# Seven block products in place of eight for the first four K-blocks of the up projection, in five of eleven column pairs of a decoder layer

## The chip, the core and the metric

The kernel runs on one core of a Trainium2 chip. The metric is the time of one execution on the device in microseconds (us). Before the change three runs took 1396.29, 1396.41 and 1396.53 us (median 1396.41).

## What is computed

One layer of a decoder on 256 tokens of width 2048: a normalisation, a combined input projection, two branches (a gated delta rule and a block attention) that sigmoid gates merge, an output projection, and then the part that matters here, a gated MLP with a short causal convolution behind its up projection:

```python
h = rms_norm(x, ln2[l])
u = causal_dwconv(h @ w_up[l], ffn_conv[l], ffn_conv_bias[l])
u_gate, u_val = jnp.split(u, 2, axis=-1)
x = x + (jax.nn.silu(u_gate) * u_val) @ w_down[l]
```

`h` is 256 x 2048, `w_up` is 2048 x 11264 (5632 columns of gate, 5632 of value), `w_down` is 5632 x 2048, all in float32.

## The kernel before

**Matrix products in three parts.** A float32 operand is split into a high and a low part that TensorE (PE) multiplies at full speed: `split` (L103) has ScalarE (ACT) write the high part with a CAST (L104) and VectorE (DVE) the low part with a TENSOR_TENSOR that subtracts (`low`, L101). A block product is then three matmuls (high times high, low of the activations times high of the weights, high times low), called products below. Each has 128 tokens x 128 K as its stationary operand and 128 K x 512 columns as its moving one. All go through `main_mm` (L93), which also counts them and, about every eight of them, calls `tick`: this lets each generator in the list `bg` record a little of its background work.

**Weights.** `fetch` (L112) loads 1 MB of a weight, 128 x 2048, through SyncE's (SP's) queue into one of four buffers `wraw`. Each half of it, 128 x 1024, is split into a slot of the ring `wh`/`wl`, which has four slots; a half in its slot is called a part here. The cast of a part waits until PE has finished with the part four places earlier, so ACT and DVE run at most three parts ahead of PE.

**Up projection (697.7 to 1161.8 us).** `by_token` (L190) makes 512 columns at a time, for both halves of the tokens, in two banks of PSUM. There are 22 such column blocks, gate and value in turn, so eleven pairs. A block has 16 K-blocks; a part holds two K-blocks, so a part gives PE 2 K-blocks x 2 token halves x 3 = 12 products, and a pair has 16 parts and 192 products. The accumulator pool has six banks as three turning pairs, and two more banks for small things.

**Behind each column block** ACT empties the two banks (`ut`, L1000), and a background generator `convolved` (L968) turns the result into channels on partitions: DVE transposes (`xt`, L468), SP issues 16 small DMAs (`uc`, L473), and then the convolution runs on each of four channel blocks, one ACT operation (L954) and two on DVE (L956). For a gate block ACT applies Silu (`sgt`, L978); for a value block (`cvf`) GpSimd (POOL) multiplies it by the gate and writes `acts`, 44 channel blocks of 128 x 256, the input of the down projection. A second generator, `residual_turned`, turns `x1`, the residual, through ACT's DMA queue.

**Down projection (from 1161.8 us).** It has 22 steps for each of two halves of the columns. In eleven of these 44 steps the function `seven` (L1035) does a 2 x 2 block product with seven block products in place of eight: DVE adds blocks of weights and of activations, the sums are split like weights, and `folds` (L1070) adds the accumulators.

**Order.** The text of the program is not the order on the engines. A scheduler places the instructions on each engine; what it chose is fixed in the program, and each engine runs its own list strictly in order, waiting by semaphores. So an instruction that waits holds up all that stand behind it on its engine.

Of the kernel before, what the change touches and what calls it, by code (L numbers as in the profile page):

```python
# [11 lines left out]
F32 = mybir.dt.float32  # L12
# [15 lines left out]
EPS = 1e-6  # L28
EVERY = 1700
SHIFT = 72  # L30
SEVEN = ([7, 10, 13, 15, 17], [2, 4, 7, 9, 12, 14])
# [34 lines left out]
def layer_kernel(ctx: ExitStack, tc: tile.TileContext, xT, xw, pos, cst, ceye, vec, convw, ffw, bdv,  # L66
# [8 lines left out]
    def r3(t, b):  # L75
        return t.rearrange("p (a b) -> p a b", b=b)
# [12 lines left out]

    spent = [0]  # L90

    def main_mm(ps, a, b, start, stop):
        r = pe.matmul(ps, a, b, start=start, stop=stop, skip_group_check=True)  # L93
# [9 lines left out]
    def split(hi, lo, src):  # L103
        casts.append(act.copy(hi, src))  # L104
        return low(hi, lo, src)
# [5 lines left out]

    def fetch(src, n=2048):  # L112
        raw = wpool.tile([P, 2048], F32, name="wraw", tag="wraw", bufs=4)
        sp.dma_start(raw[:, :n], src)
        return raw

# [8 lines left out]
    def load_w(src, o, ol=None, into=(None, None), raw=None, order=(0, 1)):  # L125
        raw = raw or fetch(src)
        w = [None, None]
        for h in order:
            w[h] = into[h] or parts(o, ol)
            lows.append(split(*w[h], raw[:, 1024 * h:1024 * h + 1024]))  # L130
        return w
# [23 lines left out]
    def mmt(name):  # L155
        return pst[0].tile([P, 2, 2, T] if wide[0] is True else [P, 2, T], F32, name=name, tag="mm")

    def sdt(name):
        return pst[1].tile([P, 512], F32, name=name, tag="sd")
# [30 lines left out]
    def by_token(ws, x, kt, name):  # L190

        if wide[0] is True:
# [743 lines left out]
    m_st.close()  # L936
    wide[0] = 2
    psum_pools(6, 2)

    b = bk.enter_context(tc.tile_pool(name="b2", bufs=2, reuse_waits="tile"))  # L940
# [19 lines left out]
    def convolved(n, ut):  # L960
# [18 lines left out]

    bg.append(residual_turned())  # L980
    pd = [None] * 8
    banks = [[2, 3, 6, 7], [0, 1, 4, 5]]

    def accumulators(n):
        for i in range(2):
            pd[n + i] = mmt("pd").rearrange("p a b -> p (a b)")

    def residual_in(p, i):
        for h in range(2):
            n = 2 * p + h  # L990
            act.copy(r3(pd[banks[p][2 * i + h]], P), x1[:, 4 * n:4 * n + 4, i * P:i * P + P])

    for n in range(NF // 2):
        if n == NF // 2 - 1:
            accumulators(2)
            residual_in(0, 0)
        ps = by_token(w_up[4 * ((n % 2) * 11 + n // 2):][:4], h2, KD, "ps_up")
        ut = ub.tile([P, 4, 2, P], F32, name="ut", bufs=2)
        for i in range(2):
            act.activation(ut[:, :, i, :], r3(ps[i], P), AF.Identity, scale=R2c[:, i:i + 1])  # L1000
        bg.append(convolved(n, ut))
    accumulators(6)
    residual_in(0, 1)
    accumulators(4)
    pd[:2] = sdt("pd"), sdt("pd")

    NQ = NF // 2
    LAST = 3
# [26 lines left out]
    def seven(c, m, q, a, raw, start, stop):  # L1035
# [6 lines left out]
        b1 = [t[:, :512] for t in b1]  # L1042
        lows.append(split(*b1, blk(raw, 0)))
        lows.append(split(*b2, raw[:, 1024:]))
        for to, more in ((0, 1), (1, 3), (3, 0), (2, 3)):
            dve.tensor_tensor(blk(raw, to), blk(raw, to), blk(raw, more), op=ALU.add)
        with tc.issue_after(lows[-1].ins):
# [3 lines left out]
        split(*s_, S)  # L1051
        split(*t13, raw[:, :1024])
        split(*t42, raw[:, 1024:])

# [31 lines left out]
    for p in range(2):  # L1086
# [3 lines left out]
        if p:  # L1090
            residual_in(1, 0)
            residual_in(1, 1)
        for q in range(NQ):
# [16 lines left out]
            for h in range(2):  # L1110
                lows.append(split(*w[h], blk(raw, h, 1024)))
            if last:
# [118 lines left out]
```

## Time and profile before

| | |
|---|---|
| median of three runs | 1396.41 us |
| the profiled execution, whole | 1396.18 us |
| its span, first to last instruction | 1394.4 us |
| granted clock of TensorE over the span | 0.999 |
| busy: PE, weight load, DVE, ACT, POOL | 99%, 86%, 74%, 57%, 10% |
| the up projection on the chain that ended last | 33% (ps_up) |

A profile page of this kind shows one execution. Busy shares are averages over very different stages; which engine sets the end is read from the chain of waits and from what PE, the busiest engine, waited for. Matmuls overlap in the records: one is listed with 380 ns, but the next begins 220 ns after it. DVE and ACT operations overlap a little as well, so their list of starts tells more than the sum of their durations.

### The profile page before, as it was taken

What the parts mean: (1) busy time and instruction counts of PE and PEld (TensorE: products, weight loads), DVE (VectorE), ACT (ScalarE), POOL (GpSimd) and SP (SyncE); (2) the same over time, 40 slices, a digit from 0 to 9 for tenths busy, and PEclk for the clock granted to TensorE, in tenths of its full rate; (3) what the DMA queues carried; (4) which work ended last, traced back from release to release, by engine and by line L of the source; (5) the groups of instructions that cost most, each with busy time, mean ns of one, the idle gap of its engine ahead of it and who ended that gap; (6) DMA issues with size and microseconds to landing.
All of it is one profiled execution on the core that took longest, in us unless ns stands there. A gap on an engine that the chain in (4) does not pass through costs nothing.

```text
span 1394.4 us, 19606 instructions
## 1 busy us (share of the span) xinstructions
PE 1384.0 (99%) x7222; PEld 1202.1 (86%) x7222; DVE 1026.5 (74%) x1500; ACT 792.9 (57%) x987; POOL 137.9 (10%) x116
## 2 busy tenths in 40 slices
PE   9999999999999999999999999999999999999997
PEld 8998899888888888889988888888888888888886
DVE  7988886988564446766756676676766667999995
ACT  6765545645466544445556555555565566666763
POOL 0021000200001100001100111100111101700000
PEclk9999999999999999999999999999999999999999
DMA  9566653576546555776557677786786776746561
GB/s 367 183 208 220 212 198 130 184 224 243 197 134 214 207 190 187 236 255 216 209 164 262 190 237 230 200 268 208 220 267 209 216 264 211 265 170 240 184 247 67
DMA packets 204673, 297.41 MB, mean 213 GB/s; under 512 B 167096, under 2 KB 169536, under 8 KB 172064
## 3 DMA queue, kind: packets, MB, share of 16 engines
q1 hardware_dynamic: 184656, 288.73, 61.5%
q10 hardware_dynamic: 17840, 3.67, 1.4%
q0 software_dynamic: 2080, 3.75, 0.9%
q8 instruction: 56, 0.92, 0.3%
q14 instruction: 41, 0.34, 0.1%
HBM read 273.48 MB, written 3.15 MB: 198 GB/s over the span
## 4 chain that ended last, share of the span: by engine, by line
PE 97%; DMA 1%; DVE 1%; SPq 0%; issue 0%; ACT 0%; DVEq 0%; ACTq 0%
PE ps_up L93 33%; PE pd L93 16%; PE ps_gate L93 12%; PE ps_gdn L93 9%; PE ps_wo L93 6%; PE ps_moba L93 6%; PE ps_br L93 5%; PE ps_v L93 3%; PE ps_z L93 3%; PE g L81 1%; DMA wraw<-in_w_o 1%; PE ps_gdn L260 1%; DMA xs<-in_xw 0%; SPq L856 0%; PE po L81 0%; PE sc L747 0%
## 5 line engine op out<-in xcount | busy, mean ns | idle before, releaser
L101 DVE TENSOR_TENSOR wl<-wraw,wh 128x1024 fp32r<-128x1024 f32 (+1 forms) x476 | 578.9, 1220 | 290.2 <-ACT wh L104 282.3
L104 ACT CAST wh<-wraw 128x1024 fp32r<-128x1024 f32 (+1 forms) x476 | 491.3, 1037 | 441.9 <-PE ps_up L93 142.2
L93 PE MATMUL ps_up<-wh,h 128*128 128x512 f32 x1408 | 422.8, 380 | 0.2 <-DVE x L916 0.2
L93 PEld LDWEIGHTS ps_up<-wh,h 128*128 128x128 f32 x1408 | 264.1, 188 | 46.0 <-issue 0.6
L93 PE MATMUL ps_up<-wl,h 128*128 128x512 f32 x704 | 267.6, 380 | 0.0
L93 PE MATMUL ps_gate<-wh,hc 128*128 128x512 f32 x512 | 155.4, 382 | 0.0
L93 PEld LDWEIGHTS ps_up<-wl,h 128*128 128x128 f32 x704 | 132.1, 188 | 22.7
L93 PE MATMUL ps_gdn<-hc,wh 128*128 128x256 f32 x720 | 124.2, 276 | 0.0
L973 POOL TENSOR_TENSOR acts<-sgt,cvf 128x256 f32<-128x256 f32 x44 | 79.3, 1812 | 448.6 <-DVE cvf L956 372.0
L93 PEld LDWEIGHTS ps_gate<-wh,hc 128*128 128x128 f32 x512 | 95.8, 188 | 16.4
L93 PEld LDWEIGHTS ps_gdn<-hc,wh 128*128 128x128 f32 x720 | 108.4, 188 | 1.3 <-issue 0.6
L93 PE MATMUL ps_gdn<-hc,wl 128*128 128x256 f32 x360 | 97.9, 275 | 0.0
L93 PE MATMUL ps_gate<-wl,hc 128*128 128x512 f32 x256 | 97.8, 382 | 0.0
L93 PE MATMUL ps_wo<-mc,wh 128*128 128x512 f32 x256 | 85.7, 379 | 0.8 <-DVE gts L886 0.8
L93 PE MATMUL pd<-tt,ah 128*128 128x512 f32 x282 | 82.2, 380 | 0.0
L93 PE MATMUL ps_moba<-wh,hc 128*128 128x512 f32 x256 | 77.1, 381 | 0.0
L93 PE MATMUL ps_wo<-mc,wl 128*128 128x256 f32 x256 | 70.5, 276 | 0.0
L93 PEld LDWEIGHTS ps_gdn<-hc,wl 128*128 128x128 f32 x360 | 67.1, 188 | 0.3
L104 ACT CAST tt<-wraw 128x1024 fp32r<-128x1024 f32 x46 | 47.4, 1045 | 33.8 <-PE pd L93 20.6
L93 PEld LDWEIGHTS pd<-tt,ah 128*128 128x128 f32 x282 | 52.9, 188 | 9.1
L93 PE MATMUL pd<-wh,ah 128*128 128x512 f32 x156 | 59.1, 380 | 0.0
L93 PE MATMUL pd<-wl,ah 128*128 128x512 f32 x156 | 59.1, 380 | 0.0
(443 smaller groups left out, 1937.1 us busy)
## 6 DMA issues: line engine op xcount, KB each, us to landing
wraw<-in_w_up SPq DMA_DIRECT2D x88, 1024.0 KB, 7.2
wraw<-in_w_dn SPq DMA_DIRECT2D x44, 1024.0 KB, 6.4
wraw<-in_w_gate SPq DMA_DIRECT2D x32, 1024.0 KB, 5.0
wraw<-in_w_gdn SPq DMA_DIRECT2D x22, 1024.0 KB, 4.9
wraw<-in_w_moba SPq DMA_DIRECT2D x16, 1024.0 KB, 6.3
wraw<-in_w_o SPq DMA_DIRECT2D x16, 1024.0 KB, 6.1
uc<-xt SPq DMA_DIRECT2D x352, 32.0 KB, 2.0
wraw<-in_w_z SPq DMA_DIRECT2D x8, 1024.0 KB, 6.9
```

The lines of the kernel that those rows point to most:

```text
L81: pe.matmul(ps, a, b, start=(start and i == 0), stop=(stop and i == n - 1), **kw)
L93: r = pe.matmul(ps, a, b, start=start, stop=stop, skip_group_check=True)
L101: return (eng or dve).tensor_tensor(lo, src, hi.bitcast(F32), op=ALU.subtract)
L104: casts.append(act.copy(hi, src))
L260: pe.matmul(ps_q0[:, b], wq[:, j, b * P:(b + 1) * P], xs[:, j], start=(j == b == 0), stop=False, skip_group_check=True)
L973: pool.tensor_tensor(acts[:, ch, :], gates[c][:, k, :], t, op=ALU.mult)
```

## The change

In column pairs 1 to 5 (of 0 to 10) the first four K-blocks are no longer done for gate and value apart, but as one 2 x 2 block product: the rows are the two halves of the tokens, the inner index is K-blocks (0, 2) against (1, 3), the columns are gate and value. Seven block products are formed in place of eight, each of two K-blocks, so 7 x 2 x 3 = 42 products in place of 48. For this the host packs these blocks of `w_up` anew; DVE adds weights (`t1`, `r11`, `t2`, `t4`, each 128 x 1024), the seven parts r10, t2, t1, r11, r20, r21 and t4 are split as other parts are, and each is used by 6 products only. The four banks of the pair (c11, c12, c21, c22) are also the scratch of the method: ACT copies c11 to `m1`, DVE makes `fold_v` and `fold_u` in spare room of `acts`, ACT copies `fold_u` back into c12, and DVE writes c22 and c21. The sums of activations, `forms`, are made once, in `combinations`. During `fewer` no background work is recorded.

All pairs now hold four banks at a time, from two sets of four (`four_banks`), and do the gate side and then the value side (`one_side`); the tile for the gates `sgt` has one buffer in place of two; the banks of the down projection are numbered anew, and its residual is copied in at once for four banks.

```diff
+UPS = (1, 2, 3, 4, 5)
...
-        if spent[0] >= EVERY:
+        if spent[0] >= EVERY and not paused[0]:
...
-            gates[c] = ub.tile([P, 4, T], F32, name="sgt", bufs=2)
+            gates[c] = ub.tile([P, 4, T], F32, name="sgt")
...
+    def part(src):
+        w = parts(60)
+        lows.append(split(*w, src))
+        return w
+
+    def products(w, them):
+        for bank, a, n, start in them:
+            for y_, x_ in ((0, 0), (0, 1), (1, 0)):
+                main_mm(fours(bank), a[x_], fours(half(w[y_], n, 512)), start and y_ + x_ == 0, False)
...
+    def fewer(ps, raw1, raw2):
+        c11, c12, c21, c22 = ps
+        fold_v, fold_u = spare(40, 2), spare(42, 2)
...
+        (r10, r11), (r20, r21) = raw1, raw2
+        t1 = ub.tile([P, 1024], F32, name="t1")
+        t4, t2 = spare(20, 4), spare(36, 4)
+        add(t1, r10, r11)
+        add(r11, r11, r21)
+        add(t2, t1, r21)
+        add(t4, t2, r20)
+        pair_of(c11, of(0, 0), part(r10), True)
+        m1 = b.tile([P, 4 * P], F32, name="m1", tag="S", bufs=1)
+        act.copy(m1, c11)
+        pair_of(c22, s6, part(t2), True)
+        dve.tensor_tensor(fold_v, c22, m1, op=ALU.subtract)
+        pair_of(c12, s5, part(t1), True)
+        dve.tensor_tensor(fold_u, c12, fold_v, op=ALU.add)
+        act.copy(c12, fold_u)
+        pair_of(c21, s7, part(r11), True)
+        dve.tensor_tensor(c22, fold_u, c21, op=ALU.subtract)
+        dve.tensor_tensor(c21, c21, fold_v, op=ALU.subtract)
+        pair_of(c11, of(1, 0), part(r20))
+        pair_of(c12, s3, part(r21))
+        pair_of(c21, of(1, 1), part(t4))
+
+    def one_side(ps, c, side, q0, to=4):
+        for q in range(q0, to):
+            raw = fetch(w_up[8 * c + 4 * side + q])
+            for h in range(2):
+                w = part(raw[h])
+                k = 4 * q + 2 * h
+                products(w, [(ps[2 * i + side], h_of(k + n, i), n, k + n == 0) for i in range(2) for n in range(2)])
...
+    for c in range(NU):
+        ps = four_banks("ps_up")
+        if c in UPS:
+            paused[0] = True
+            fewer(ps, fetch(w_up[8 * c]), fetch(w_up[8 * c + 4], spare(24, 8)))
+            paused[0] = False
+        one_side(ps, c, 0, c in UPS)
+        evicted(c, ps, 0)
+        one_side(ps, c, 1, c in UPS, 4 - (c == NU - 1))
+        if c < NU - 1:
+            evicted(c, ps, 1)
```

The scheduler then sets the order on each engine. Three places in pair 3 show it. The line numbers are those of the kernel in question; `wh_61` and `wl_62` are the ring, and in the changed kernel `acts_6142` is the spare room that holds r20, r21, t2, t4 and the folds.

On DVE before, between the parts of one column block there stand convolution steps (`sgt`) and the low parts of the same weights:

```order
L101 TENSOR_TENSOR wl_62<-wraw_6787,wh_61 128x1024 x2
L468 STREAM_TRANSPOSE xt_6761<-ut_6740 128x1024
L956 SCALAR_TENSOR_TENSOR sgt_6826<-uc_6592,ffv_5500,sgt_6826 128x255
L101 TENSOR_TENSOR wl_62<-wraw_6830,wh_61 128x1024
L956 SCALAR_TENSOR_TENSOR sgt_6826<-uc_6592,ffv_5500,sgt_6826 128x254
L101 TENSOR_TENSOR wl_62<-wraw_6830,wh_61 128x1024
```

On DVE now, in `fewer` of pair 3, from the low part of t2 to the two folds that write c22 (`ps_up_7093`) and c21 (`ps_up_7092`):

```order
L102 TENSOR_TENSOR wl_62<-acts_6142,wh_61 128x1024
L102 TENSOR_TENSOR wl_62<-t1_7099,wh_61 128x1024
L102 TENSOR_TENSOR wl_62<-wraw_7096,wh_61 128x1024
L102 TENSOR_TENSOR wl_62<-acts_6142,wh_61 128x1024
L1047 TENSOR_TENSOR acts_6142<-ps_up_7093,m1_7112 128x512
L102 TENSOR_TENSOR wl_62<-acts_6142,wh_61 128x1024
L1049 TENSOR_TENSOR acts_6142<-ps_up_7095,acts_6142 128x512
L102 TENSOR_TENSOR wl_62<-acts_6142,wh_61 128x1024
L102 TENSOR_TENSOR wl_62<-wraw_7167,wh_61 128x1024
L470 STREAM_TRANSPOSE xt_7179<-ut_7089 128x1024
L1052 TENSOR_TENSOR ps_up_7093<-acts_6142,ps_up_7092 128x512
L1053 TENSOR_TENSOR ps_up_7092<-ps_up_7092,acts_6142 128x512
```

The folds into c22 and c21 stand behind the low part of the first ordinary part (`wraw_7167`, called n1 below) and behind a transpose of the pair before.

On ACT before, two `cvf` operations of the convolution stand between casts of parts:

```order
L104 CAST wh_61<-wraw_6663 128x1024 x2
L473 DMA x1_5499<-xr_6451 32x8x32
L954 ACTIVATE cvf_6678<-uc_6428,ffv_5500 128x256
L954 ACTIVATE cvf_6691<-uc_6428,ffv_5500 128x256
L104 CAST wh_61<-wraw_6709 128x1024
```

On ACT now, in pair 3, from the copy of c11 to the copy of `fold_u` into c12 (`ps_up_7095`):

```order
L1045 COPY m1_7112<-ps_up_7094 128x512
L105 CAST wh_61<-acts_6142 128x1024 x2
L105 CAST wh_61<-wraw_7167 128x1024
L475 DMA x1_5499<-xr_6533 32x8x32
L956 ACTIVATE cvf_7173<-uc_6839,ffv_5500 128x256
L956 ACTIVATE cvf_7189<-uc_6839,ffv_5500 128x256
L1050 COPY ps_up_7095<-acts_6142 128x512
L105 CAST wh_61<-wraw_7167 128x1024
```

The copy into c12 stands behind the cast of n1 and two convolution operations.

On PE now, in pair 3, from the first two products of n1 into c11 (`ps_up_7094`) over the six of r21 into c12 to the first of t4 into c21 (before, PE did 12 products of each part in a row):

```order
L94 MATMUL ps_up_7094<-wh_61,h2_5401 128x4x32x4 x2
L94 MATMUL ps_up_7095<-wh_61,ah_6145 128x4x32x4
L94 MATMUL ps_up_7095<-wh_61,al_6146 128x4x32x4
L94 MATMUL ps_up_7095<-wl_62,ah_6145 128x4x32x4
L94 MATMUL ps_up_7095<-wh_61,ah_6145 128x4x32x4
L94 MATMUL ps_up_7095<-wh_61,al_6146 128x4x32x4
L94 MATMUL ps_up_7095<-wl_62,ah_6145 128x4x32x4
L94 MATMUL ps_up_7094<-wl_62,h2_5401 128x4x32x4
L94 MATMUL ps_up_7094<-wh_61,h2_5401 128x4x32x4 x2
L94 MATMUL ps_up_7094<-wl_62,h2_5401 128x4x32x4
L94 MATMUL ps_up_7094<-wh_61,h2_5401 128x4x32x4 x2
L94 MATMUL ps_up_7092<-wh_61,h2_5401 128x4x32x4 x2
```

Ahead of these rows stand the 30 products of r10, t2, t1, r11 and r20; six products of n1 and two of the next part have been drawn ahead of t4.

More of the change, by code (lines that the diff above doesn't have):

```diff
@@ L110, in layer_kernel, with fetch @@
     lows, casts = [], []
[L112 to L115, printed above, removed]
+    def fetch(src, raw=None):
+        if raw is None:
+            raw = wpool.tile([P, 2048], F32, name="wraw", tag="wraw", bufs=4)
+        sp.dma_start(raw, src)
+        return [raw[:, 1024 * h:1024 * h + 1024] for h in range(2)]
     ring = [wpool.tile([P, 4, 1024 + 64], F32R, name=t, bufs=1) for t in ("wh", "wl")]
@@ L978, in convolved @@
             act.activation(gates[c], gates[c], AF.Silu)
[L980 to L997, printed above, removed]
+    NU = NF // 4
@@ new lines, in layer_kernel, with combinations @@
+    forms = [[b.tile([P, 2 * T + 64], F32R, name=t, tag=t)[:, 8:8 + 2 * T] for t in ("ah", "al")] for _ in range(2)]
+    def combinations():
+        raw = acts[:, 40:44, :]
+        sums = acts[:, 36:40, :].rearrange("p k t -> p (k t)").rearrange("p (f j t) -> p f j t", f=4, t=P)
+        for k in range(4):
+            act.activation(raw[:, k, :], x1[:, k, :], AF.Identity, scale=ln2v[:, k:k + 1])
+        a11, a12, a21, a22 = (raw[:, e::2, i * P:i * P + P] for i in range(2) for e in range(2))
+        s7, s5, s6, s3 = (sums[:, n] for n in range(4))
+        yield
+        dve.tensor_tensor(s7, a11, a21, op=ALU.subtract)
+        dve.tensor_tensor(s5, a21, a22, op=ALU.subtract)
+        yield
+        dve.tensor_tensor(s6, a22, s7, op=ALU.add)
+        dve.tensor_tensor(s3, a12, s6, op=ALU.subtract)
+        for n, (hi, lo) in enumerate(forms):
+            yield
+            split(hi, lo, sums[:, 2 * n:2 * n + 2].rearrange("p f j t -> p (f j t)"))
@@ new lines, in fewer, with of, pair_of, add @@
+    def fewer(ps, raw1, raw2):
+        c11, c12, c21, c22 = ps
+        fold_v, fold_u = spare(40, 2), spare(42, 2)
+        def of(k, i):
+            return [h_of(k + 2 * j, i) for j in range(2)]
+        def pair_of(bank, a, w, start=False):
+            products(w, [(bank, a[j], j, start and j == 0) for j in range(2)])
+        s7, s5, s6, s3 = ([combined(n, j) for j in range(2)] for n in range(4))
+        def add(to, one, other):
+            dve.tensor_tensor(to, one, other, op=ALU.add)
+        (r10, r11), (r20, r21) = raw1, raw2
[19 more added lines that the diff above has]
+        pair_of(c21, of(1, 1), part(t4))
@@ L999, in layer_kernel, with four_banks @@
         for i in range(2):
[L1000 to L1005, printed above, removed]
+            act.activation(ut[:, :, i, :], r3(ps[2 * i + n], P), AF.Identity, scale=R2c[:, i:i + 1])
+        bg.append(convolved(2 * c + n, ut))
+    turned = [0]
+    def four_banks(name):
+        turned[0] ^= 1
+        t = [mmt(name).rearrange("p a b -> p (a b)") for _ in range(4 if turned[0] else 2)]
+        return [t[n] for n in (0, 2, 1, 3)] if turned[0] else [sdt(name) for _ in range(2)] + t
@@ new lines, in residual_in @@
+    def residual_in(p):
+        for j in range(4):
+            n = 2 * p + j % 2
+            act.copy(r3(pd[banks[p][j]], P), x1[:, 4 * n:4 * n + 4, j // 2 * P:(j // 2 + 1) * P])
+    bg.append(combinations())
+    bg.append(residual_turned())
+    for c in range(NU):
[9 more added lines that the diff above has]
+            evicted(c, ps, 1)
@@ L1007, in layer_kernel @@
+    pd = four_banks("pd")
+    banks = [[0, 1, 2, 3], [4, 5, 6, 7]]
+    residual_in(0)
+    one_side(ps, NU - 1, 1, 3)
+    evicted(NU - 1, ps, 1)
+    pd += four_banks("pd")
     NQ = NF // 2
@@ L1042, in seven @@
         b1 = [t[:, :512] for t in b1]
-        lows.append(split(*b1, blk(raw, 0)))
-        lows.append(split(*b2, raw[:, 1024:]))
+        lows.append(split(*b1, blk(raw[0], 0)))
+        lows.append(split(*b2, raw[1]))
+        r4 = [blk(r, n) for r in raw for n in range(2)]
         for to, more in ((0, 1), (1, 3), (3, 0), (2, 3)):
-            dve.tensor_tensor(blk(raw, to), blk(raw, to), blk(raw, more), op=ALU.add)
+            dve.tensor_tensor(r4[to], r4[to], r4[more], op=ALU.add)
         with tc.issue_after(lows[-1].ins):
```

36 lines of the change are left out of this document (25 added, 11 removed).

## The prediction

> **What bounds the kernel now.** I read the page first, then the chain that ended last in order of time, then what PE waited for in the two stages from the output projection on.
>
> ```profile
> span 1394.4 us, 19606 instructions
> PE 1384.0 (99%) x7222; PEld 1202.1 (86%) x7222; DVE 1026.5 (74%) x1500; ACT 792.9 (57%) x987; POOL 137.9 (10%) x116
> ...
> 696.88 0.70 DVE x L916
> 697.58 0.14 issue
> 697.71 5.77 PE ps_up L93 x25
> 703.49 0.34 PE R L81 x4
> 703.82 457.96 PE ps_up L93 x2081
> 1161.79 225.09 PE pd L93 x1023
> ...
> engine line waited for: us in total, times, longest us
> PE ps_wo L93 <- DVE gts L886: 0.8, 1, 0.8
> PE ps_up L93 <- DVE x L916: 0.2, 1, 0.2
> ```
>
> From 697.7 us to 1161.8 us the chain is nothing but the up projection's products, and PE waits 0.2 us in all: this stage lasts as long as its products. One costs 457.96 / 2081 = 0.220 us, and in the down projection 225.09 / 1023 = 0.220 us. So each product taken out is worth 0.22 us, as long as PE goes on without waiting. The question is whether its helpers keep up. By stage (about one pair each, the third row a part of the down projection):
>
> ```profile
> 822.40:864.00 41.60, 41.60 (x191) 35.49 (x190) 28.70 (x35) 24.03 (x29) 5.02 (x4) 1.00 0.74 226
> 864.00:905.60 41.60, 41.60 (x191) 35.49 (x190) 28.82 (x34) 23.69 (x30) 5.02 (x4) 1.00 0.76 233
> 1162.00:1270.00 108.00, 108.00 (x493) 92.15 (x492) 102.90 (x139) 73.52 (x98) 27.50 (x4) 1.00 0.65 236
> ```
>
> The columns are the stage's length, then the busy time of PE, weight load, DVE, ACT and POOL. In 41.60 us DVE has 28.8 us of work and ACT 23.9. The last row matters as much: the down projection does the same kind of block product with DVE busy 102.90 of 108 us, and PE still never waits. DVE work alone does not stop PE; its place in time can.
>
> **What is removed.** Pairs 1 to 5 lose 6 products each: 5 x 6 x 0.22 = 6.6 us, the most that the change can bring.
>
> **What is added, by amount.** Per changed pair: three parts more (19 for 16), four adds of 128 x 1024 and four folds of 128 x 512 on DVE; three casts and two copies on ACT.
>
> ```profile
> L101 DVE TENSOR_TENSOR wl<-wraw,wh 128x1024 fp32r<-128x1024 f32 x176 | 217.4, 1236 | 139.9 <-ACT wh L104 136.1 <-PE ps_up L93 2.3 <-DMA uc<-xt 1.4
> L301 DVE TENSOR_TENSOR sq<-sq,sq 128x1024 f32<-128x1024 f32 x1 | 1.2, 1218 | 0.0
> L1080 DVE TENSOR_TENSOR pd<-pd,fu 128x512 f32<-128x512 f32 x4 | 2.8, 688 | 0.0
> L104 ACT CAST wh<-wraw 128x1024 fp32r<-128x1024 f32 x177 | 185.2, 1047 | 156.0 <-PE ps_up L93 142.2 <-DMA wraw<-in_w_up 7.9 <-DMA uc<-xt 2.1
> L991 ACT COPY pd<-x x8: 580/584/591, 1117.7 to 1267.7; 128x512 f32<-128x512 f32 x8
> ```
>
> DVE: 3 x 1.236 + 4 x 1.218 + 4 x 0.688 = 11.3 us, so 28.8 + 11.3 = 40.1 us of busy time in a pair of 186 x 0.22 = 40.9 us. ACT: 3 x 1.047 + 2 x 0.584 = 4.3, so 28.2. Both fit, DVE barely.
>
> **What is added, by place.** Within `fewer` a part feeds PE for 6 x 0.22 = 1.32 us where an ordinary one feeds it for 2.64. The adds can be made early, since both raw weights come long before. Seven low parts and four folds cannot: the ring lets a part be cast only when the part four before it is done, and the folds need products. I follow pair 3 by hand. The spacings come from the starts in the timelines (start, duration, engine):
>
> ```profile
> 906.63 0.38 PE L93 MATMUL ps_up<-wl,h 128*128 128x512 f32 x1
> 907.95 0.38 PE L93 MATMUL ps_up<-wl,h 128*128 128x512 f32 x1
> 907.05 0.69 ACT L1000 ACTIVATE ut<-ps_up,R2c 128x512 f32<-128x512 f32 x1 [0.49 <-PE ps_up L93]
> 908.15 1.05 ACT L104 CAST wh<-wraw 128x1024 fp32r<-128x1024 f32 x1 [0.41 <-PE ps_up L93]
> 914.44 1.58 ACT L954 ACTIVATE sgt<-uc,ffv 128x256 f32<-128x256 f32 x3
> 916.12 1.05 ACT L104 CAST wh<-wraw 128x1024 fp32r<-128x1024 f32 x1
> 921.12 1.06 ACT L978 ACTIVATE sgt<-sgt 128x1024 f32<-128x1024 f32 x1 [1.30 <-DVE wl L101]
> 922.08 1.03 ACT L104 CAST wh<-wraw 128x1024 fp32r<-128x1024 f32 x1
> 909.23 1.23 DVE L101 TENSOR_TENSOR wl<-wraw,wh 128x1024 fp32r<-128x1024 f32 x1 [1.42 <-ACT wh L104]
> 910.37 1.24 DVE L468 STREAM_TRANSPOSE xr<-x 128x1024 f32<-128x1024 f32 x1
> 911.53 0.44 DVE L956 SCALAR_TENSOR_TENSOR sgt<-uc,ffv,sgt 128x255 f32<-128x255 f32 x1
> 911.89 1.24 DVE L468 STREAM_TRANSPOSE xt<-ut 128x1024 f32<-128x1024 f32 x1
> 1172.63 0.68 DVE L101 TENSOR_TENSOR al<-acts,ah 128x512 fp32r<-128x512 f32 x1
> 1173.24 2.35 DVE L101 TENSOR_TENSOR wl<-wraw,wh 128x1024 fp32r<-128x1024 f32 x2
> ```
>
> A low part or a transpose is followed by the next DVE operation after 1.14 to 1.16 us, one of 512 elements after 0.61 (1172.63 to 1173.24), a convolution step after about 0.4; these I use, not the durations. ACT goes on 0.96 us after an operation of 1024 elements (921.12 to 922.08) and 0.56 after one of 256 (1.68 for three). A result in PSUM can be read 0.42 us after its last product began (906.63 to 907.05), which is 0.20 after the 0.22 that it takes; a ring slot is free just as its last product ends (907.95 + 0.22 = 908.17, cast at 908.15). From DVE to PE a handoff costs 0.14 (697.58 to 697.71, above).
>
> Time zero is the first product of pair 3. ACT casts r11 at 0.0, r20 at 1.76 (r10 done, PE having mixed it with t2), copies `m1` at 2.72, casts r21 at 3.2, t4 at 4.2, n1 at 5.28 (r11 done); then come two `cvf` (6.24, 6.80), and only then the copy into c12: 7.33 to 7.91. DVE: low r20 at 2.83, `fold_v` 3.97, low r21 4.58, `fold_u` 5.72, low t4 6.33, low n1 7.47, transpose 8.61, c22 9.77, c21 10.38 to 11.07.
>
> PE has done its first 30 products at 6.60 and two of n1 at 7.04. Then r21 waits for the copy into c12, until 8.04: **1.0 us lost**, and all that stands behind it waits, since it is the same queue. Six products and six drawn-ahead ones bring it to 10.68, where t4 waits for the fold of c21, until 11.20: **0.5 us**. So pair 3 loses 1.5 us and saves 1.32.
>
> The same steps for the others, in their own orders:
> - Pair 1: no convolution ahead of the copy, folds right behind low t4 (c21 ready at 8.67, needed at 8.36): 0.3 us.
> - Pair 2: three adds stand right ahead of the low parts, and PE takes t1 between the products of t2, so t2's slot is free at 4.40 only and r21 is cast then, n1 at 5.36; two `cvf` and a further cast (7.38) put the copy at 8.34 to 8.92. On DVE low r21 begins at 5.9, `fold_u` 7.04, low n1 7.64, a transpose 8.78, two convolution steps, c22 10.74, c21 11.34 to 12.03. r21's products wait from 7.04 to 9.06, t4's from 11.7 to 12.17: 2.0 + 0.5 = 2.5 us.
> - Pair 4: two `cvf` and the next part's cast (7.35) ahead of the copy, 8.26 to 8.84, so r21's products wait from 7.04 to 8.98: 1.9 us; c21, ready at 10.84, is wanted at 11.6.
> - Pair 5: two `cvf` ahead of the copy (7.9): 1.0 us; folds in time.
>
> Sum of the waits 0.3 + 2.5 + 1.5 + 1.9 + 1.0 = 7.2 us. Behind `fewer` the parts last 2.64 us again against about 1.14 on DVE, twelve times a pair, which leaves 12 x 1.5 = 18 us for some 9 us of background work: I take it that the next pair finds the ring full again.
>
> **What costs nothing, I think.** `combinations` and its two splits run in the output projection, where PE waited 0.8 us once; the first extra 1 MB load is issued behind the residual's loads, and the weights behind it are wanted about 10 us later. One `sgt` buffer in place of two makes ACT wait for POOL at most while three parts of 2.64 us lie ahead of PE. Banks in fours, ordinary pairs and the change to the down projection: the same products with the same helpers. Bounds for all of it together: 0, and 0.8 us (the largest wait of PE in these stages) for either border of the stage, so 1.6; I take 0, since PE waits nowhere between.
>
> **Sum.** 1396.18 (the profiled execution; span 1394.4 and 1.8 around it) - 6.6 + 7.2 = **1396.8 us**, 0.4 above the median of 1396.41.
>
> [...] In all stages above the granted clock is 1.00.
>
> ```profile
> 609.00:613.00 4.00, 3.43 (x21) 3.15 (x22) 3.96 (x6) 1.49 (x2) 0.00 (x0) 1.00 1.01 422
> ```
>
> Here PE stood still for 0.57 us and kept the clock. [...]
>
> **Rivals.**
> 1. **The waits are mostly hidden; faster.** If ACT gets through its two `cvf` and the copy in time, only DVE's folds count. Pairs without the convolution in the way lose 0.3 (pair 1): 1396.18 - 6.6 + 5 x 0.3 = 1391.1. For it: the down projection's seven-product steps never stop PE. Against it: there the products go to banks of their own and are folded once at the end; here c12 and c21 must be folded within the run.
> 2. **DVE comes late into each pair; slower.** From the last ordinary part on, the queue of pairs 2 and 3 runs without a gap. If neighbours do not overlap as in the rows above (1.236 for 1.14, 0.688 for 0.61), twelve low parts and folds take about 12 x 0.09 = 1.1 us longer, and every pair waits that much more: 1396.8 + 5 x 1.1 = 1402.3. It decides where r20's low part starts later than about 3.5 us into the pair.
> [...]
>
> That the change does not do what it says I exclude: the order has 42 products in each of the five pairs.
>
> **How the numbers follow.** My forecast, gain and waits within 2.8 us of each other (0.2% of the time, about what a measurement of this kernel can tell from no change), gets 0.43. Rival 1, faster by more than that, 0.27; rival 2 0.27; rival 3 0.03. So faster 0.27, same 0.43, slower 0.30. The forecast's own range is 1393.6 to 1399.2. For 8 in 10 I reach down to rival 1's time, 1391, and up to rival 2's, 1402.5; left out are no waits at all (1389.6) and rival 3.
>
> **What would show it.** PE's list of waits should name, in pairs 1 to 5 alone, ACT's copy into c12 (the L1050 line) and DVE's fold of c21 (L1053), together about 7 us, with single waits of 1 to 2 us in pairs 2 to 4 and nearly none in pair 1. Products should number 2082 at 0.22 us. ACT should show two `cvf` between n1's cast and the copy. I am wrong if PE waits instead for low parts, if it waits in ordinary pairs, or if its waits add up to under 4 or over 10 us.

## The result, and the profile after

The changed kernel takes **1404.96 us** (median of 4 runs, 1402.90 to 1405.11) against 1396.47 for the kernel before on the same chip: a ratio of **1.0055, 95% interval 1.0037 to 1.0072**. It is slower, by 8.2 us more than forecast and beyond the range's upper end of 1402.5. The profiled execution, on which the account below rests, took 1402.9 us and is the fastest of the four.

The page of the changed kernel, and its list of what PE waited for from the up projection on (us in total, times, longest):

```profile
span 1401.1 us, 19676 instructions
PE 1383.0 (99%) x7192; PEld 1197.4 (85%) x7192; DVE 1081.1 (77%) x1561; ACT 809.0 (58%) x1018; POOL 128.9 (9%) x116
...
PE ps_up L94 <- ACT ps_up L1050: 4.4, 4, 1.6
PE pd L94 <- ACT wh L105: 3.0, 1, 3.0
PE ps_up L94 <- DVE ps_up L1053: 0.9, 2, 0.7
PE ps_up L94 <- DVE wl L102: 0.8, 1, 0.8
PE ps_up L94 <- DVE x L918: 0.2, 1, 0.2
```

Before, only the last of these stood there. 30 products are gone (7192 for 7222), DVE has 54.6 us more work. The waits on L1050 and L1053 were forecast; the other two were not. The 3.0 us stand at the border to the down projection. The timeline of PE there (start, duration, idle time before in brackets), and the same stretches by engine, where the column behind the five engines is the granted clock:

```profile
1162.33 0.40 PE L94 MATMUL ps_up<-wl,h 128*128 128x512 f32 x1
1165.78 1.18 PE L94 MATMUL pd<-wh,ah 128*128 128x512 f32 x4 [3.05 <-ACT wh L105]
...
1169.55 0.63 PE L94 MATMUL pd<-wl,ah 128*128 128x512 f32 x1
1169.97 0.63 PE L94 MATMUL pd<-wh,al 128*128 128x512 f32 x1
...
1171.70 0.38 PE L94 MATMUL pd<-wh,al 128*128 128x512 f32 x1
...
1165.70:1169.20 3.50, 3.34 (x10) 2.36 (x11) 3.47 (x5) 3.50 (x6) 0.00 (x0) 0.73 1.00 419
```

PE stands still for 3.05 us; then products follow each other at 0.42 us in place of 0.22 (1169.55 to 1169.97) until about 1170.8, and the granted clock reads 0.73 over that window (1.00 up to 1167.30 us, 0.50 from there to 1170.71, 1.00 behind it).

Where the 6.7 us between the two spans (1401.1 and 1394.4) come from, I counted from the starts of the products: whatever lies between two starts beyond 0.22 us is time lost. By that count a wait is some 0.3 us more than in the list, which starts behind the earlier product's 0.38 us and leaves out the slower restart (behind the wait in pair 2 the second product begins 0.34 us after the first, 788.26 to 788.60).

| us | before | after | difference |
|---|---|---|---|
| start of the stage | 697.71 | 696.68 | -1.0 |
| products taken out, 30 x 0.22 | | | -6.6 |
| lost in pairs 0 to 5 | 0.5 | 7.9 | +7.4 |
| lost in pairs 6 to 10 | 0 | 1.0 | +1.0 |
| border, PE idle | 0 | 3.2 | +3.2 |
| first 30 products behind it | 0 | 2.2 | +2.2 |
| rest of the down projection | -0.1 | 0.3 | +0.4 |

The sum is +6.6. The first half of it, -6.6 and +7.4, is the forecast's; the lower half, 6.8 us, is what it costed at nothing.

What the border waited for is seen two steps back. ACT in the changed kernel:

```profile
1156.94 1.05 ACT L105 CAST wh<-wraw 128x1024 fp32r<-128x1024 f32 x1
1164.19 0.60 ACT L956 ACTIVATE sgt<-uc,ffv 128x256 f32<-128x256 f32 x1 [6.20 <-DMA uc<-xt]
1164.70 1.98 ACT L105 CAST wh<-wraw 128x1024 fp32r<-128x1024 f32 x2
```

The casts of the first down weights stand in ACT's queue behind a convolution step, and that waits 6.2 us for its 16 `uc` transfers, which SP issues between the weight loads. SP's queue (start, time from the first issue to the last), first before, then after:

```profile
1095.26 5.63 SPq L114 DMA_DIRECT2D wraw<-in_w_up  x4
1102.11 13.48 SPq L473 DMA_DIRECT2D uc<-xt  x16
1115.69 6.31 SPq L114 DMA_DIRECT2D wraw<-in_w_up  x4
1123.23 11.87 SPq L473 DMA_DIRECT2D uc<-xt  x16
```

```profile
1098.70 3.90 SPq L116 DMA_DIRECT2D wraw<-in_w_up  x4
1103.82 16.39 SPq L475 DMA_DIRECT2D uc<-xt  x16
1120.31 3.91 SPq L116 DMA_DIRECT2D wraw<-in_w_up  x4
1125.44 15.80 SPq L475 DMA_DIRECT2D uc<-xt  x16
```

Before, SP spends 5.6 to 6.3 us on four loads: it is early and waits until a raw buffer comes free for the fourth. Afterwards that wait is some 2 us shorter, since SP comes later, and the next 16 transfers take 16 us. Their waits say why; SP's list for the up stage, before and after:

```profile
SPq L114 <- DVE wl L101: 116.4, 35, 5.3
SPq L473 <- DMA wraw<-in_w_up: 43.0, 31, 3.0
```

```profile
SPq L116 <- DVE wl L102: 94.9, 34, 7.2
SPq L475 <- DMA wraw<-in_w_up: 57.2, 31, 2.8
```

A `uc` transfer has no data in common with a weight load, yet waits for it, 31 times before, for 43.0 us. The program has transfers of both kinds report their landing on the same semaphore (completion counter), for which the later one waits. Before, for example, the load issued at 910.48 us has number 107 in the trace and landed at 919.86, and the `uc` transfer next on 107 was issued at 919.88. ACT's `xr` transfers report there too: the one issued at 911.64 has number 108 and landed at 920.06, and the `uc` transfer next on 108 was issued at 920.51. The reading to be tested is a loop (theory S): loads issued late go out together, are still in flight when the 16 `uc` transfers come, hold them up, and so make the next loads late. The first row of each pair is SP's slack; it shrank from 116 to 95 us.

These two sums do not foretell the loss by themselves: e1 below, without a changed pair, has less slack (91.3 us) and more of the other wait (75.8 us) than the change, and its border is clean. What goes with the border is how long SP's loads pause there, from the last load of one group to the first of the next, around the last 16 `uc` transfers (here 1143.84 to 1162.82, 19.0 us). Of the twenty kernels of this document, ten have 9.6 to 14.4 us there, and their border itself idles nothing (the 5.2 us of e11 below lie behind it); ten have 15.4 to 19.0 us, and theirs idles 0.9 us or more. In e1 the pause between groups rises to 20.6 us in pair 6 and is back at 14.1 us by the border; in the change it rises to 20.0 us and does not fall below 17.3 again.

### The profile page after: what moved, and what is told of

The parts are those of the page before. It is cut to its first block, busy times and chain, and to the rows that moved or that the text cites. A ratio compares the mean times of both kernels' runs of the same rounds, so it can differ in the third digit from the quotient of the medians.

```text
span 1401.1 us, 19676 instructions
## 1 busy us (share of the span) xinstructions
PE 1383.0 (99%) x7192; PEld 1197.4 (85%) x7192; DVE 1081.1 (77%) x1561; ACT 809.0 (58%) x1018; POOL 128.9 (9%) x116
## 5 line engine op out<-in xcount | busy, mean ns | idle before, releaser
L102 DVE TENSOR_TENSOR wl<-wraw,wh 128x1024 fp32r<-128x1024 f32 x466 | 564.0, 1221 | 218.1 <-ACT wh L105 214.2
L105 ACT CAST wh<-wraw 128x1024 fp32r<-128x1024 f32 x466 | 478.2, 1036 | 380.5 <-PE ps_gate L94 62.0
L94 PE MATMUL ps_up<-wh,h 128*128 128x512 f32 x1308 | 390.1, 381 | 1.1 <-DVE ps_up L1053 0.9
L94 PEld LDWEIGHTS ps_up<-wh,h 128*128 128x128 f32 x1308 | 245.1, 188 | 44.7 <-DVE ps_up L1053 2.1
L94 PE MATMUL ps_up<-wl,h 128*128 128x512 f32 x654 | 245.1, 380 | 0.8 <-DVE wl L102 0.8
L94 PEld LDWEIGHTS ps_up<-wl,h 128*128 128x128 f32 x654 | 122.8, 188 | 22.6 <-DVE wl L102 1.4
L975 POOL TENSOR_TENSOR acts<-sgt,cvf 128x256 f32<-128x256 f32 x44 | 70.4, 1608 | 444.0 <-DVE cvf L958 402.0
```

The lines of the kernel that those rows point to most:

```text
L102: return (eng or dve).tensor_tensor(lo, src, hi.bitcast(F32), op=ALU.subtract)
L975: pool.tensor_tensor(acts[:, ch, :], gates[c][:, k, :], t, op=ALU.mult)
```

## The experiments

A ratio is to the kernel before on the same chip, with its 95% interval. "Lost" is the count of the table above, from one profile each: in pairs 0 to 5 (0.5 of it is there before too), in pairs 6 to 10, at the border with the 30 products behind it, and in the rest of the down projection. Two profiles are of executions far from the median: e13's took 1405.85 us, and e14's, 1397.70, is its slowest.

| run | us | ratio | lost |
|---|---|---|---|
| e1 no pair | 1396.61 | 0.9994 (0.9985 to 1.0003) | 0.5, 1.2, 0, 0 |
| e2 folds first | 1408.72 | 1.0083 (1.0070 to 1.0095) | 7.9, 6.8, 2.8, 2.4 |
| e3 two gates | 1404.62 | 1.0051 (1.0039 to 1.0063) | 7.3, 3.1, 4.3, 1.8 |
| e4 early xr | 1404.60 | 1.0064 (1.0038 to 1.0090) | 8.3, 3.5, 2.0, 1.9 |
| e5 no xr (work left out) | 1393.79 | 0.9974 (0.9964 to 0.9985) | 4.4, 0, 0, 1.6 |
| e6 uc by GpSimd | 1422.90 | 1.0178 (1.0164 to 1.0192) | 6.5, 0, 0, 27.5 |
| e7 pairs 1, 3, 5 | 1404.37 | 1.0047 (1.0034 to 1.0060) | 12.0, 0, 1.6, 0 |
| e8 sums by GpSimd | 1406.96 | 1.0066 (1.0052 to 1.0079) | 11.7, 1.6, 3.3, 2.2 |
| e9 xr by GpSimd | 1400.14 | 1.0035 (1.0013 to 1.0057) | 6.7, 0, 1.5, 2.3 |
| e10 uc by GpSimd, pairs 0 to 5 | 1410.04 | 1.0086 (1.0073 to 1.0099) | 6.3, 9.9, 4.6, 0.3 |
| e11 e9 and e10 | 1419.21 | 1.0151 (1.0138 to 1.0164) | 4.8, 14.1, 5.2, 6.9 |
| e12 no pair, xr by GpSimd | 1395.80 | 0.9982 (0.9974 to 0.9991) | 0.5, 0, 0, 0 |
| e13 order, xr by GpSimd | 1402.38 | 1.0045 (1.0030 to 1.0060) | 7.2, 5.1, 4.2, 1.2 |
| e14 one pair, xr by GpSimd | 1395.84 | 0.9990 (0.9981 to 0.9998) | 0.8, 0, 0, 1.0 |
| e15 pairs 1, 3, 5, order | 1405.48 | 1.0059 (1.0046 to 1.0071) | 12.3, 0, 1.6, 0.5 |
| e16 xr early | 1397.05 | 0.9995 (0.9986 to 1.0003) | 8.1, 0, 0, 1.1 |
| e17 no pair, xr early | 1395.25 | 0.9980 (0.9971 to 0.9989) | 0.5, 0, 0, 0 |
| e18 xr early, copy first | 1397.98 | 0.9998 (0.9989 to 1.0007) | 8.6, 1.5, 0, 0 |

### Which part of the change costs the rest: e1 to e4

e1, the new structure without a changed pair:

```diff
-UPS = (1, 2, 3, 4, 5)
+UPS = ()
```

> No pair is done with 42 products (UPS empty), so 30 more products run than in the change, 2112 in the up stage as before; the pairs in four banks, the single sgt buffer, the new code order and the combinations (computed, not used) stay. Theory A (the 8 us above the forecast come from the five pairs, whose late casts and loads reach into the pairs behind them): no wait on the fold lines, the border from the up to the down projection idles under 0.5 us, no product at half clock there; 1396.5 us, within 1.0. Rival B (the structure alone, the sgt buffer above all, starves the pairs and the border): the border idles about 3 us again and then runs 3.4 us at half clock; 1396.4 - 1.0 + 3.2 + 2.5 + 1 = about 1402.

Theory A, against rival B: 1396.61, no pause at the border. Banks in fours, the single `sgt` buffer and the new order are worth nothing together, though a wait of 1.0 us in the seventh pair, the same that the change has, offsets a stage that starts 1.2 us earlier. All 8 us need the five pairs; whether they need something else besides, e5 and e16 say.

e2, the folds ahead in their queues (the low parts of r20 and r21 queued behind `fold_v` and `fold_u`; the next cast, conv steps and low part behind the copy and the fold of c21):

```diff
-        act.copy(c12, fold_u)
+        cp = act.copy(c12, fold_u)
...
-        pair_of(c11, of(1, 0), part(r20))
-        pair_of(c12, s3, part(r21))
+        pair_of(c11, of(1, 0), part(r20, [v_]))
+        pair_of(c12, s3, part(r21, [u_]))
...
+        casts.append(cp)
+        after[:] = [cp, f_]
```

> In the five pairs the copy of c12 on ACT comes ahead of the next cast and of the conv steps, and on DVE the folds come ahead of the low parts that stood before them; nothing else changes. Theory A: of the 7.3 us of waits on the copy and on the fold of c21 at most 2.5 stay, so the time falls by about 5 us, to 1400 (1398.5 to 1401), if the border still pauses; if the border is cured by it too, 1394.5. Rival (the low parts that are now behind the folds become what PE waits for, the ring of four parts being empty): the waits stay near 7 us under another name, and the time at 1405, within 1.0.

The rival, and worse. PE's waits in e2 (L1059 is the fold of c21 there):

```profile
PE ps_up L94 <- DVE wl L102: 5.9, 7, 1.3
PE ps_up L94 <- DVE ps_up L1059: 2.2, 4, 0.7
PE pd L94 <- ACT wh L105: 2.1, 1, 2.1
```

The waits for the copy are gone and low parts have taken their place: pairs 0 to 5 lose 7.9 us as in the change, and pairs 6 to 10 lose 6.8 us where the change lost 1.0. This order of the queues is not what the five pairs lack.

e3, and below it e4 (in `residual_turned`):

```diff
-            gates[c] = ub.tile([P, 4, T], F32, name="sgt")
+            gates[c] = ub.tile([P, 4, T], F32, name="sgt", bufs=2)
...
-        t1 = ub.tile([P, 1024], F32, name="t1")
+        t1 = spare(32, 4)
```

```diff
-        yield from wait(26)
+        yield from wait(4)
```

> The gate tile sgt has two buffers again, as before (t1 moves into a spare piece of acts to make room); the five pairs are as in the change. Rival B1 (one sgt buffer holds up ACT until GpSimd has multiplied with the old gate, and everything behind that is late): the wait in the seventh pair and the border's pause go, 1398.5 us (1397.5 to 1400). Theory A with the shared queues: ACT's four waits of 9.7 us for GpSimd go, but the border still idles about 3 us; 1404.5, within 1.0.

> The transposes of x1 (residual_turned) start 22 steps earlier, so that their 64 small transfers on ACT's queue end near 1097 us and not at 1134; all else is as in the change. Theory C (the transfers on ACT's queue beside the last weight loads make ACT and SP wait for each other, and the delay reaches the border): the border idles under 1 us, no half clock; 1399.5 us (1398.5 to 1401). If those transfers have no part in it: 1405, within 1.0, with the border idle about 3 us.

Neither moves the time. In e3 the border still idles 2.8 us, so the one `sgt` buffer is not the cause. In e4 the border's pause shrinks to 1.5 us and the half clock goes (2.0 us lost there and in the 30 products behind, 5.4 in the change), yet pairs 6 to 10 lose 3.5 us: the lost time changes its place and stays. Something behind PE seems to keep its own pace.

### The loop on SP: e5, e6, e9, e10, e11

e5 and e6:

```diff
-    bg.append(residual_turned())
```

```diff
-                        ub.tile([P, 8, P], F32, name="xt"), sp, 4, 1)
+                        ub.tile([P, 8, P], F32, name="xt"), pool, 4, 1)
```

> Leaves out the turning of x1 (residual_turned: 4 x 16 small transfers on ACT's queue and their transposes), so the residual added at the end is not turned; all else is as in the change. Theory S (a loop on SP's in-order queue: the 16 transfers of uc wait for weight loads still in flight, so the next loads are issued late and all at once, and are in flight together when the next 16 come; the xr transfers lengthen it): in pairs 6 to 10 the long interval between two weight loads falls from 17.5 to 20 us to about 15.5, the border idles under 0.5 us with no half clock, and of the waits only those in the five pairs stay, 7.3 us: 1397.3 (1395.5 to 1399). Rival (xr has no part in it, the five pairs alone make everything late): 1403 or more, the border idle as long.

> The 16 transfers of uc of each side are issued by GpSimd and no longer by SP, which then issues nothing but weight loads in the up stage; all else is as in the change. Theory S: the loads are no longer held behind uc and stay spread out at about 5.3 us, the border idles under 0.5 us, and the waits in the five pairs stay as they are: 1397 (1395.5 to 1399). Rival (GpSimd's queue is in order too, so the products with the gate now stand behind the transfers and the convolutions come late, or the transfers take longer from there): 1405 or more.

Without the 64 `xr` transfers nothing is lost from pair 6 to the border, and the kernel is at 0.9974. SP's waits in e5:

```profile
SPq L116 <- DVE wl L102: 130.5, 45, 7.2
SPq L475 <- DMA wraw<-in_w_up: 29.0, 19, 3.3
```

SP has slack again and `uc` waits for loads half as long as in the change. The pairs lose 3.9 us (4.4 less 0.5), 3.5 less than in the change, more than expected; of that the four transposes and 64 issues left out on DVE and ACT may be a part, which e5 cannot tell apart. In e6 SP issues loads only, ten of them 5.3 us apart (47.96 / 9):

```profile
1083.11 47.96 SPq L116 DMA_DIRECT2D wraw<-in_w_up  x10
```

Pairs 6 to 10 and the border lose nothing there either: theory S as far as the up stage goes. The time as a whole is the rival's. What PE waited for in e6, and GpSimd's queue:

```profile
PE pd L94 <- ACT ah L105: 9.2, 1, 9.2
...
1223.72 1.53 POOL L975 TENSOR_TENSOR acts<-sgt,cvf 128x256 f32<-128x256 f32 x2 [2.50 <-DVE cvf L958]
1225.42 9.21 POOL L475 DMA_DIRECT2D uc<-xt  x16 [0.18 <-DVE S L1150]
1241.17 1.51 POOL L975 TENSOR_TENSOR acts<-sgt,cvf 128x256 f32<-128x256 f32 x2 [6.54 <-DVE cvf L958]
```

The products with the gate stand behind `uc` in one queue; the last are made at 1245 us, and the down projection waits for its inputs.

e9 moves only xr to GpSimd (`act, 1, 3` becomes `pool, 1, 3`), e10 only the `uc` transfers of pairs 0 to 5 (`pool if n < 12 else sp`), e11 both:

> The 64 small transfers of xr are issued by GpSimd and no longer by ACT; their transposes on DVE and their bytes stay, and so does everything else of the change. Theory S1 (the xr transfers harm by their place in ACT's queue and by the completion counters that they share with SP's transfers, so that SP's uc transfers wait longer for loads in flight): as in e5 the loads spread out again behind pair 6, the border doesn't pause, the waits left are some 3 us in pairs 2 to 5 and 1 us in the down projection: 1394.5 (1393 to 1396.5). Rival S2 (it is the traffic and DVE's transposes of xr themselves): 1402 or more, with long intervals of 17.5 to 20 us between loads in pairs 6 to 10.

> GpSimd issues the uc transfers of pairs 0 to 5 only; SP issues those of pairs 6 to 10 as before. In e6 the up stage itself lost only 3.1 us to waits, and the 23 us came in the down projection, where GpSimd's products with the gate were late by whole pairs. Theory S: waits of about 3 us in pairs 2 to 5, loads spread from there on, border and down projection without pauses: 1396.6 - 6.6 + 3.1 = 1393.1 (1392 to 1396). Rival (GpSimd's lag from the first six pairs is still there at the border, or the loads bunch again within pairs 6 to 10): 1400 or more.

> e9 and e10 together: GpSimd issues xr's transfers and the uc transfers of pairs 0 to 5. Theory S1: not slower than the better of the two, 1393 (1391.5 to 1395.5). Rival (GpSimd's queue is too full with both: the products with the gate, behind transfers in its order, come late): slower than e9 by 2 us or more.

e9 has 1.0035 where the change has 1.0055, with intervals that overlap; its profile loses nothing in pairs 6 to 10 and idles 0.9 us at the border. Its twelve executions spread widely, from 1397.18 to 1413.90 us, four of them above 1404. It lies between S1 and S2: queue and counters seem to be a part, not all. e10 and e11 have the rivals' times. In e10 it is less GpSimd's lag than the loads again: from 1030 us to the border ACT waits 24.2 us for `uc` transfers, which SP issues there, and 8.1 us for GpSimd's products.

### What a changed pair is worth: e7, e8, e12 to e18

e7 has `UPS = (1, 3, 5)`; e8:

```diff
-        add(t2, t1, r21)
-        add(t4, t2, r20)
+        pool.tensor_tensor(t2, t1, r21, op=ALU.add)
+        pool.tensor_tensor(t4, t2, r20, op=ALU.add)
```

> Only pairs 1, 3 and 5 are done with 42 products, with an ordinary pair between them; 12 more products than in the change, 18 fewer than in e1. Theory (the lead of the low parts over the products, about 6 us, is used up in a changed pair and comes back in an ordinary pair behind it): the three pairs wait 0.3 + 0.8 + 0.8 us against 4.0 saved, and the border doesn't pause: 1394.5 (1393.5 to 1396). Rival (the loads once late stay late over an ordinary pair too, so the second and third pair start without lead): 1397.5 or more, with waits of 1.5 to 2.5 us in pairs 3 and 5 and some at the border.

> Two of the four sums of weight blocks in each of the five pairs (t2 and t4, 2.8 us of DVE together) run on GpSimd; all else is as in the change. Theory D (in a changed pair DVE has more to do than the products last, about 15 us against 9.2, and the folds are late for that): the waits on c12's copy and on the fold of c21 fall from 7.3 us to under 4, and the time to 1401 (1399 to 1402.5). Rival (the folds are late because of what stands ahead of them in the queue, not for the amount of work; or the sums come later from GpSimd and PE waits for them): 1404.5 or more.

Both have the rivals' times. With room between them three pairs lose more, 12.0 us up to pair 5, than five in a row; 6.5 us of it stand in the ordinary pairs 2 and 4, where neither theory nor rival of e7 had a wait. e8 does cut the waits on the copy (2.8 us in PE's list for 4.4), but 6.4 us go to low parts. The mechanism is seen best in e15, which repeats e7 with other orders and xr on GpSimd; DVE ahead of pair 3 there (L1043 are the sums):

```profile
804.98 0.44 DVE L958 SCALAR_TENSOR_TENSOR cvf<-uc,ffv,cvf 128x254 f32<-128x254 f32 x1
811.41 1.23 DVE L1043 TENSOR_TENSOR t<-wraw 128x1024 f32<-128x1024 f32 x1 [6.00 <-DMA wraw<-in_w_up]
812.56 1.22 DVE L102 TENSOR_TENSOR wl<-wraw,wh 128x1024 fp32r<-128x1024 f32 x1
...
816.75 1.22 DVE L102 TENSOR_TENSOR wl<-wraw,wh 128x1024 fp32r<-128x1024 f32 x1
```

The sums for the next changed pair stand in DVE's queue ahead of the last low parts of the pair before. When the load that they need is late, DVE stands still for 6.0 us with work for PE behind it, and PE waits 2.4 and 0.8 us. So a late load hurts twice: the changed pair that needs it, and by its sums the pair ahead of that.

With xr on GpSimd: e12 has no changed pair, e14 pair 1 alone, e13 all five with e2's order (t4's low part behind the fold of c21 as well) and, within a part, the four products with the high part ahead of the two with the low part; e15 has e13's edits in pairs 1, 3, 5.

> e1 (no pair with 42 products) with xr's transfers on GpSimd: what the queue alone is worth. If moving the queue cures only the lateness behind the changed pairs, e1's one wait of 1.1 us in the seventh pair goes and nothing else: 1395.5 (1394.8 to 1396.5), and e9 beats it only by what the five pairs earn net, 6.6 less some 4.5 of waits, about 2 us or less. If it is worth more by itself, 1394.5 or less, the change earns nothing even so.

> Only pair 1 is done with 42 products, and xr's transfers are on GpSimd: the price of one changed pair against e12. Theory: 6 products less, 1.3 us, and a wait of some 0.3 us in pair 1, nothing late behind it since SP has slack there: 1.0 us faster than e12, ratio to before 0.9975 (0.9965 to 0.9985). Rival (one pair already bunches the loads and the next pairs wait): 0.9985 or more.

> All five pairs as in the change, with xr's transfers on GpSimd (e9), the copy of c12 and the folds ahead of the low parts and casts that stood before them (e2, and the low part of t4 behind the fold of c21 too), and within a part of a changed pair the four products with the high part ahead of the two with the low part. Theory: both costs are real and separate; the waits in the pairs fall from e9's 5.3 us to under 2, and the loads stay spread: 3 us faster than e9, 0.998 of the kernel before (0.996 to 1.000). Rival (SP's loop over loads and uc can't go faster than the products in a changed pair, so what the pairs gain is lost behind them, as in e2): not faster than e9, ratio 1.003 or more, with waits in the pairs behind 5 or at the border.

> Pairs 1, 3 and 5 with 42 products, with e13's order and xr's transfers on GpSimd. Theory: 4.0 us saved, under 1.5 us of waits in the three pairs, and the ordinary pairs between let the loads spread again: 2.5 us faster than e12, ratio 0.9965 (0.995 to 0.998). Rival (SP's loop as in e7, where pairs 2 and 4 waited for low parts): 0.9985 or more, with waits in pairs 2 and 4.

e12 loses nothing beyond the start of the stage and beats the kernel before. e14 is no faster than e12 (0.9990 and 0.9982, the rival's time): its pair waits 0.3 us as forecast for pair 1 and saves 1.3. Behind it the loads go out together, but no pair waits for them, which the rival had expected; the down projection loses 1.0 us to late low parts of `acts`. Neither e13 nor e15 is faster than e9, as the rivals had it.

e16, e17 and e18 issue xr early. The expectations have nearly all of it in pair 0; in the traces 31 or 32 of the 64 transfers are issued there, and the last at 780 to 794 us, in pair 2:

```diff
-        yield from wait(26)
+        yield from wait(6)
...
-            yield from turn(r3(blk, P), blk, ub.tile([P, 8, P], F32, name="xr"), act, 1, 3)
+            yield from turn(r3(blk, P), blk, ub.tile([P, 8, P], F32, name="xr"), pool, 4, 0)
```

> The change with xr's 64 transfers issued by GpSimd within some 40 us from the start of the up stage, nearly all of them in pair 0, when no uc transfer is on the way yet; nothing is left out. Theory S: as in e5 (which left xr out) the loads spread again behind the five pairs, the border doesn't pause, and the waits left are about 3.5 us in the pairs and 1 us in the down projection: ratio to the kernel before 0.9975 (0.996 to 0.999). Rival (e5 was faster for the DVE and ACT work that it left out, not for the transfers between uc and the loads): 1.001 or more.

> The same without any pair of 42 products, as e1 and e12: what is left for the five pairs once xr is out of the way. Theory: no waits at all in the up stage, as in e12, ratio 0.9985 (0.9975 to 0.9993), so that the five pairs earn 1 to 2 us in e16 (6.6 saved, some 4.5 lost to waits). If they earn nothing even here, e17 is as fast as e16 or faster.

> e16 with the copy of c12 on ACT ahead of the next pair of casts and conv steps behind it in the code (DVE's order untouched). In e5 the copy stood behind one cast and two conv steps and PE waited 0.8 us for it in each of pairs 2 to 5. Theory: in these pairs the wait falls to under 0.3 us where the copy moves, 2 us in all, and since the loads are not late it is earned: ratio 0.996 (0.9945 to 0.9975). Rival (SP's loop limits the pairs and takes it back, as in e2): no faster than e16.

e17, with SP at 7.65 us for four loads and 11.78 for 16 `uc`, is with e12 (0.9980 and 0.9982) the fastest of all that do the whole work, and it has **no changed pair**; its theory, that e16 is the faster by 1 to 2 us, failed:

```profile
1092.42 7.65 SPq L116 DMA_DIRECT2D wraw<-in_w_up  x4
1101.29 11.78 SPq L475 DMA_DIRECT2D uc<-xt  x16
```

e16 adds the five pairs to it. The border is clean, pairs 6 to 10 lose nothing, and still it is 1.8 us slower by the medians (1397.05 and 1395.25): the pairs lose 7.6 us more than e17's where they save 6.6, and the down projection loses 1.2 more. So of e16's expectation the half behind the pairs came true, with nothing left out, and the half inside them did not: they lose 8.1 us where 3.5 were expected, and the ratio falls between theory and rival.

```profile
PE ps_up L94 <- ACT ps_up L1050: 3.0, 4, 1.2
PE ps_up L94 <- DVE ps_up L1053: 0.7, 1, 0.7
PE ps_up L94 <- DVE wl L102: 0.7, 2, 0.4
PE pd L94 <- DVE al L102: 0.5, 1, 0.5
```

e18 gains nothing over e16, as its rival had it; that SP's loop is the reason, as the rival says, is not shown. In pair 3 the copy (L1056) still stands behind a cast, and its input, DVE's L1055, comes only at 830.42 + 0.68 us, behind the low parts:

```profile
830.42 0.68 DVE L1055 TENSOR_TENSOR acts<-ps_up,acts 128x512 f32<-128x512 f32 x1
...
831.03 1.04 ACT L105 CAST wh<-wraw 128x1024 fp32r<-128x1024 f32 x1 [1.20 <-PE ps_up L94]
831.98 0.58 ACT L1056 COPY ps_up<-acts 128x512 f32<-128x512 f32 x1
```

## Why the prediction was wrong

- **What is removed**: right; 2082 products of the up projection at 0.22 us, 6.6 us.
- **The waits in the five pairs**: right, place by place. Followed by hand: 0.3, 2.5, 1.5, 1.9 and 1.0, sum 7.2. Measured by the starts: 0.3, 2.4, 1.9, 1.9 and 0.9, sum 7.3. PE named L1050 and L1053 as foretold. One wait was mis-sized: in pair 3 that for c21 was 1.0 us by the starts and not 0.5, as DVE began the low part of r20 at 3.24 us into the pair, 0.4 later than followed.
- **"What costs nothing, I think": the step that failed.** It took 0, with a bound of 1.6 us, for everything outside `fewer`, and the sentence ahead of it took "that the next pair finds the ring full again". The trace of the change has 6.8 us there: 1.0 in pairs 6 to 10, 3.2 idle at the border, 2.2 behind it, 0.4 later; less the 1.0 us by which the stage starts earlier, that is nearly all of the 6.1 us between forecast and profiled execution. Nor was the ring full within the five: from the end of the first low part of a pair to its first product there were 5.6 and 5.0 us in pairs 1 and 2, and 1.6 to 1.8 us in pairs 3 to 5. The waits there came out right all the same, since ACT kept its predicted times (in pair 3 the copy into c12 at 7.21 us for 7.33). Ordinary pairs do have DVE time enough by the forecast's account, 12 x 1.5 us a pair; what they lack is early loads. e1 shows that the paragraph is right about the time of the structure by itself; e5, e6 and e16 that the loss in pairs 6 to 10 and at the border goes once transfers are taken out of the way of SP's loads, with the five pairs unchanged. So the loss at the border takes both, the five pairs and xr's transfers. That the way from one to the other leads through the completion counters is argued: no run changes the counters alone.
- **Why the bound was too small**: it was taken from PE's largest wait, 0.8 us. A PE that never waits says nothing of how near its helpers are to being late. It can be counted, from the end of a low part to the first product of its part: in pairs 8 to 10 the shortest such time is 4.8 us before, 0.3 to 0.8 us in the change, 0.9 to 4.3 us in e1 and 3.1 to 3.8 us in e16. SP's list of before also had a hint: 116.4 us of waiting for free buffers over 22 sides is some 5 us of slack a side of 21.1 us, and for 43.0 us `uc` waited for loads that it has nothing to do with. I read neither.
- **Rival 1** (hidden waits, 1391.1) is out. **Rival 2** (1402.3) has the nearest time, not the mechanism: the waits inside the pairs are not longer than followed by hand.
- **Rival 3** has a chance of 0.03. A pause that costs clock enters neither the forecast nor rivals 1 and 2, and the trace of the change has one: behind the 3.05 us at the border the granted clock is 0.50 (1167.30 to 1170.71 us), and the first 30 products there lose 2.2 us. Behind the 1.63 us in pair 2 it stays at 1.00 (787 to 794 us).
- **The signs**: two of the three conditions under which I would be wrong were set well. PE waited in an ordinary pair and for low parts there.

Left open: the three unprofiled runs of the change are 2.0 to 2.2 us longer than the profiled one. e2, e3 and e4 show that lost time turns up in other places when little is moved, but those three were not looked into. Open too is why the five pairs lose 3.5 us less in e5 than in the change: e16, which moves the transfers and leaves nothing out, has no such gain, but a part of its xr still falls into pairs 1 and 2. A rival was not tested: no background work is recorded during `fewer`, and xr's last transfer goes out at 1134.4 us in the change, at 1077.1 before and at 1075.5 in e1. No run takes away that pause in the recording alone; e4, with the last at 1097.5, has half the idle time at the border.

## What to carry to other kernels

When a kernel waits nowhere, measure place by place how far its helpers are ahead (from the end of a helper's result to its first use, and how long the loads pause between groups) before giving them more to do. How long the load queue waits for free buffers in all is a hint to its slack and no more: e1 had less of it than the change and lost nothing at the border. A transfer in an in-order queue can wait for another that it has no data in common with (the `uc` transfers for weight loads, 57.2 us in the change), so look for such rows among the waits of the DMA queues. Where moving a wait brings no time, and it comes back under another name, test a kernel that leaves the suspected traffic out, and then one that only moves it: e5 pointed at once to what e2, e3 and e4 had not, and e16 told the traffic from the work left out.

## What the runs showed of the hardware that was not expected

In e10 a pause far shorter than the one at the border, 1.20 us for 3.05, is followed by a granted clock of 0.56. PE around 872 us:

```profile
871.81 0.49 PE L94 MATMUL ps_up<-wh,ah 128*128 128x512 f32 x1 [1.20 <-ACT ps_up L1050]
872.14 0.38 PE L94 MATMUL ps_up<-wh,al 128*128 128x512 f32 x1
...
873.03 0.63 PE L94 MATMUL ps_up<-wh,al 128*128 128x512 f32 x1
873.46 0.63 PE L94 MATMUL ps_up<-wl,ah 128*128 128x512 f32 x1
...
873.00:876.40 3.40, 3.40 (x10) 2.69 (x9) 3.40 (x6) 1.05 (x1) 1.99 (x4) 0.56 1.07 268
```

1.20 us idle, three products that begin 0.33, 0.23 and 0.23 us ahead of the next, then products 0.43 us apart from 872.60 to 876.02 us, at a granted clock of 0.56 in the window above. In the change itself 1.63 us in pair 2 cost no clock (granted 1.00 from 787 to 794 us). At the border, with the 30 products behind it, e8 loses 3.3 us around a pause of 2.56 us, and e13 4.2 us around a shorter one of 2.07, behind which its products follow each other at 0.43 us. The length of a single pause does not decide it in these traces; what does was not shown.
